# The memory's norm and transposes computed early, stored feature-major in DRAM and reloaded at the end of the mixers

## The chip, the cores and the metric

The kernel runs on one core of one Trainium2 chip. The metric is the device time of one execution in microseconds; each kernel is run three times and the median counts. A profile is one more execution, recorded by the chip's profiler.

## The reference

Two blocks run after each other on 512 tokens of width 1024, in fp32. The first block has two layers of four mixers (gated linear recurrences, a gated delta rule and a latent attention), an output projection and a gated feed-forward network (FFN). The second block has a layer A and a layer B, and each of them has, beside its own attention, a memory attention over 256 tokens `mem` that do not depend on anything the first block computes:

```python
def memory_attention(qm, mem, l, mem_norm, mem_w_kv, mem_q_norm, mem_k_norm):
    kvm = rms_norm_2(mem, mem_norm[l]) @ mem_w_kv[l]
    km, vm = jnp.split(kvm, 2, axis=-1)
    km = rms_norm_2(km.reshape(B, M, MEM_HEADS, MEM_HEAD_DIM), mem_k_norm[l])
    ...
```

Here M is 256, the width of `mem` is 1024, and `mem_w_kv[l]` is 1024 x 512. What the change touches is the first line: the norm of `mem`, and its transposition into the layout in which TensorE can multiply it with `mem_w_kv`.

## The kernel before

A product of fp32 matrices is made of three fp32r products: each operand is split into a high part `hi` (a ScalarE copy to fp32r) and the rest `lo` (a VectorE subtraction), and hi·hi, lo·hi and hi·lo are added in PSUM. Weights arrive by DMA into `wr` (512 KB each), ScalarE casts them to `wh`, VectorE subtracts to `wl`. Activations are split the same way after a transpose on TensorE (`tr`, into the PSUM pool `psS` or `psD`). All DMAs are issued by SyncE (SP), one after the other.

Every operation is first recorded, in program order, and then a planner sets a fixed order on each engine by list scheduling: among the operations that it takes to be ready it prefers the one that comes first in the program, and it gives each tile a slot of its pool (`p4w` has 16 slots of 4 KB a partition, `p4h` 8, `p4p` 8, `wr` 2, `wh` 4, `wl` 4, `psA` 3, `psS` 3, `psD` 2). The chip then runs each engine's list in that order. All recorded instructions carry the line of the helper that emits them, L328, so they are told apart by their tiles. SP's list is fixed in the same way, so a DMA that waits for its data holds up those behind it.

A first_block layer l (`layer1`) runs: `next_norm` with the first three weights of `w_in` (`fm_first`), then the mixers as a list of items in the order gdn, gate_d, hgrn, gla, mla, gate_a, gate_b, mem, then the output projection with `w_out`, then `next_norm` and `ffn`. The items `mem` come last. They prepare the memory of second-block layer l: `mem_h` loads the norm's gain row and the two 128-token tiles of `mem` (512 KB each), normalizes each (`norm_tok`: a ScalarE square with accumulation, four small POOL operations for the pair, a VectorE scale by row and gain), transposes it (8 TensorE transposes per tile into two `psS` tiles) and splits what comes out (a ScalarE copy and a VectorE subtraction of 512 columns per `psS` tile). Then `i_tm` multiplies with `mem_w_kv`: two token tiles of keys and two of values, each with 24 matmuls of 256 columns, 96 in all. `away` stores keys and values to DRAM (`md`), and layers A and B fetch them with `mem_back`.

Of the kernel before, what the change touches and what calls it, by code (L numbers as in the profile page):

```python
# [10 lines left out]
F32 = mybir.dt.float32  # L11
F32R = mybir.dt.float32r
U32 = mybir.dt.uint32
I32 = mybir.dt.int32
AF = mybir.ActivationFunctionType
# [132 lines left out]
def run(gen):  # L148
    for _ in gen:
        pass  # L150
# [463 lines left out]
class Net:  # L614
    def __init__(self, ctx, tc, I, out, dbg=None, upto=None):
# [20 lines left out]
        self.pps = {"A": pool("psA", 3, space=PSUM), "S": pool("psS", 3, space=PSUM), "D": pool("psD", 2, space=PSUM)}  # L636
        self.pdr = pool("pdr", 2, space=bass.MemoryType.DRAM)
        self.turn = 0
        self.ready_w, self.mem_kv = {}, {}
        self.ahead = lambda: None  # L640

    def nm(self, s):
# [1227 lines left out]
    def ffn(self, l, h, rest, then):  # L1870
# [13 lines left out]
            return self.fm(h, w)  # L1884

        for f in range(NF):
            psg, psu = proj(2 * f), proj(2 * f + 1)
            c = self.p2()
            self.act(c, psg, AF.Copy, scale=self.fcols[l](f, 2))
            for j in (1, 0):  # L1890
                s = 2 - j
                self.stt(c[:, s:], psg[:, :S - s], self.fcols[l](f, j), c[:, s:], ALU.mult, ALU.add)
            self.act(c, c, AF.Gelu_apprx_tanh)
            self.mul(c, psu, c)
            a = self.p4([128, 2, S], F32R, "w" if f < 16 else "p")
            self.split(a[:, 0, :], a[:, 1, :], c)
            acts.append(a)
# [6 lines left out]
    def layer1(self, l, steps):  # L1904
# [12 lines left out]
        gla, gate_b = self.gla_items(l, W, h, TB)  # L1917
        mla = self.mla_items(l, W, h, TC)
        mem = self.mem_items(l)
        self.merge(self.project(gdn + gate_d + hgrn + gla + mla + gate_a + gate_b + mem))  # L1920
        gb = self.bcast_row(I["post_mix_g"][l], D)
        mt = self.mixT
# [88 lines left out]
                self.mul(self.rot[:, i, t].rearrange("p w (b d) -> p w b d", b=2), g4,  # L2011
                         tab[:, t * 8:(t + 1) * 8].unsqueeze(1).unsqueeze(1).broadcast_to([128, 2, 2, 8]), self.G)

    def mem_h(self, l, h):

        I = self.I
        gb = self.bcast_row(I["mem_norm_2"][l], D)
        h.extend([self.p4([128, 4, 256], F32R) for _ in range(2)] for _ in range(2))
        for t in range(2):
            xn = self.p4()  # L2020
            raw = self.p4()
            self.SP.dma_start(out=raw, in_=I["mem_2"][0, t * 128:(t + 1) * 128, :])
            self.norm_tok(raw, gb, xn)
            yield self.when(xn)
            for g in range(2):
                ps = self.ps("S")
                for k in range(4):
                    self.tr(ps[:, k * 128:(k + 1) * 128], xn[:, (g * 4 + k) * 128:(g * 4 + k + 1) * 128])
                self.split(h[0][g][:, :, t * 128:(t + 1) * 128], h[1][g][:, :, t * 128:(t + 1) * 128],
                           ps.rearrange("p (k n) -> p k n", k=4))  # L2030

    def mem_items(self, l):

# [490 lines left out]
```

## Time and profile before

| what | us |
| --- | --- |
| three runs | 2032.98, 2035.56, 2035.82 (median 2035.56) |
| the profiled execution | 2033.99 |
| its span | 2032.2 |
| TensorE (PE) busy in it | 1954.1 (96%), mean granted clock 0.987 |
| VectorE (DVE) busy | 1250.3 (62%) |
| ScalarE (ACT) busy | 946.6 (47%) |
| GpSimd (POOL) busy | 265.7 (13%) |

The span is the part of the profiled execution in which instructions run; the other 1.8 us lie around it. Busy times of engines overlap. PEclk is the granted clock of TensorE as a share of its full 2.4 GHz; 0.50 is its lower level, 1.2 GHz. In a row of the timeline, the number in brackets is the time for which the engine stood idle before the instruction, and behind the arrow stands what released it. Consecutive matmuls of one kind share one row (x8), and their ends are modelled, so starts are the safer numbers.

### The profile page before, as it was taken

To read this page: it belongs to the slowest core of one execution; us is meant where nothing else is said; L and a number is where in the kernel's file an instruction comes from. 1 tells how busy PE (TensorE), PEld (TensorE's weight loads), DVE (VectorE), ACT (ScalarE), POOL (GpSimd) and SP (SyncE) were. 2 spreads that over 40 slices of the span, in tenths; PEclk is the share of its full clock that TensorE was granted. 3 is DMA by queue.
4 is the path that set the end of the run, shared out by engine and by line. 5 is a ranking of instruction groups with operands and counts; after the bars stand their busy time and mean duration, and the time that the engine had idled before them with its cause. 6 is when DMAs were issued, how large, how long until landed. Compare 5 with 4: busy or idle time off the path is not lost.

```text
span 2032.2 us, 33173 instructions
## 1 busy us (share of the span) xinstructions
PE 1954.1 (96%) x13254; PEld 1655.6 (81%) x13254; DVE 1250.3 (62%) x2319; ACT 946.6 (47%) x1715; POOL 265.7 (13%) x362
## 2 busy tenths in 40 slices
PE   7999989899999989998898999999999999999999
PEld 6888778788888878887787888888899988888787
DVE  7688873544442257878836444422548886558796
ACT  5744463433332236633634333322446774457782
POOL 3101111000000021011201000000223220005131
PEclk9999989999999999999999999999999999999999
DMA  5321224433332433302243333324331213421121
GB/s 166 97 63 36 83 81 138 125 94 94 98 99 94 155 90 96 92 24 68 82 152 112 100 94 94 99 97 167 121 89 43 84 63 114 135 84 55 60 74 62
DMA packets 231305, 191.62 MB, mean 94 GB/s; under 512 B 22352, under 2 KB 201200, under 8 KB 231152
## 3 DMA queue, kind: packets, MB, share of 16 engines
q1 hardware_dynamic: 231152, 189.51, 30.4%
q8 instruction: 104, 1.70, 0.3%
q14 instruction: 49, 0.40, 0.1%
HBM read 174.28 MB, written 15.20 MB: 93 GB/s over the span
## 4 chain that ended last, share of the span: by engine, by line
PE 84%; DVE 7%; ACT 3%; POOL 2%; issue 2%; DMA 1%; SPq 1%; DVEq 0%; ACTq 0%; POOLq 0%
PE psA L328 63%; PE psS L328 12%; PE psD L328 9%; DVE p4w L328 5%; POOL st L328 2%; ACT p4w L328 1%; DVE p4p L328 1%; DVE wl L328 1%; SPq L328 1%; DVE p L328 1%; ACT wh L328 0%; DMA wr<-in_w_in_dram 0%; ACT p4p L328 0%; ACT p L328 0%; DVE p4h L328 0%
## 5 line engine op out<-in xcount | busy, mean ns | idle before, releaser
L328 PE MATMUL psA<-p4h,wh 128*128 128x512 f32 (+1 forms) x2144 | 627.9, 377 | 14.3 <-DVE p4h L328 7.1
L328 DVE TENSOR_TENSOR wl<-wr,wh 128x1024 fp32r<-128x1024 f32 (+6 forms) x304 | 349.0, 1152 | 413.7 <-ACT wh L328 408.4
L328 ACT CAST wh<-wr 128x1024 fp32r<-128x1024 f32 (+6 forms) x304 | 298.5, 990 | 465.2 <-PE psA L328 279.8
L328 PEld LDWEIGHTS psA<-p4h,wh 128*128 128x128 f32 x2144 | 393.5, 191 | 89.9 <-DVE p4h L328 8.3
L328 PE MATMUL psA<-p4h,wl 128*128 128x512 f32 (+1 forms) x1072 | 400.6, 374 | 0.0
L328 PE MATMUL psA<-wh,p4h 128*128 128x256 f32 (+1 forms) x1792 | 353.8, 289 | 0.9 <-DVE p4h L328 0.7
L328 PEld LDWEIGHTS psA<-wh,p4h 128*128 128x128 f32 x1792 | 282.3, 188 | 6.6 <-issue 2.0
L328 PE MATMUL psA<-wl,p4h 128*128 128x256 f32 (+1 forms) x896 | 257.5, 288 | 0.4 <-DVE wl L328 0.4
L328 PEld LDWEIGHTS psA<-p4h,wl 128*128 128x128 f32 x1072 | 204.3, 191 | 37.0
L328 POOL TENSOR_SCALAR st<-st 128x1 f32<-128x1 f32 (+4 forms) x108 | 46.1, 427 | 1310.6 <-ACT p4w L328 908.5
L328 PEld LDWEIGHTS psA<-wl,p4h 128*128 128x128 f32 x896 | 168.8, 188 | 2.6 <-DVE wl L328 0.8
L328 PE MATMUL psA<-wh,p4w 128*128 128x512 f32 (+1 forms) x540 | 159.4, 368 | 0.0
L328 ACT ACTIVATE p<-p 128x512 f32<-128x512 f32 (+2 forms) x174 | 87.3, 526 | 100.2 <-DVE p L328 98.9
L328 POOL TENSOR_TENSOR st<-st,c 128x1 f32<-128x1 f32 (+4 forms) x106 | 115.4, 1090 | 8.0
L328 ACT ACTIVATE p4w<-psA 128x256 f32<-128x256 f32 (+5 forms) x138 | 61.6, 452 | 107.0 <-PE psA L328 105.9
L328 PEld LDWEIGHTS psA<-wh,p4w 128*128 128x128 f32 x540 | 96.6, 188 | 18.2 <-issue 0.5
L328 PE MATMUL psS<-consts,p4w 128*128 128x128 f32 (+1 forms) x448 | 70.5, 291 | 36.7 <-DVE p4w L328 28.9
L328 PE MATMUL psS<-p4w,p4w 128*64 128x64 f32 (+9 forms) x800 | 94.6, 271 | 5.3 <-DVE p4w L328 5.1
L328 PE MATMUL psA<-wl,p4w 128*128 128x512 f32 (+1 forms) x270 | 98.5, 365 | 0.0
L328 PE MATMUL psS<-wh,p4w 128*128 128x512 f32 x300 | 97.3, 395 | 0.0
L328 DVE TENSOR_TENSOR p<-psA,p 128x512 f32<-128x512 f32 x54 | 37.3, 691 | 95.8 <-PE psA L328 94.2
L328 PEld LDWEIGHTS psS<-consts,p4w 128*128 128x128 f32 x448 | 54.5, 153 | 47.7 <-issue 19.1
(227 smaller groups left out, 3105.0 us busy)
## 6 DMA issues: line engine op xcount, KB each, us to landing
wr<-in_w_in_dram SPq DMA_DIRECT2D x44, 512.0 KB, 3.8
wr<-in_ffn_w_gate_dram SPq DMA_DIRECT2D x44, 512.0 KB, 3.8
wr<-in_ffn_w_up_dram SPq DMA_DIRECT2D x44, 512.0 KB, 3.8
wr<-in_ffn_w_down_dram SPq DMA_DIRECT2D x44, 512.0 KB, 3.5
wr<-in_w_out_dram SPq DMA_DIRECT2D x16, 512.0 KB, 4.7
wr<-in_a_w_in_dram SPq DMA_DIRECT2D x16, 512.0 KB, 3.8
wr<-in_b_w_in_dram SPq DMA_DIRECT2D x16, 512.0 KB, 3.9
p4w<-xd SPq DMA_DIRECT2D x12, 512.0 KB, 4.4
```

The costliest lines, as they stand in the source:

```text
L328: op.fn(*op.args, **op.kw)
```

## The change

The norm and the transposes of the memory move out of `mem_h` into a new function `mem_prep(l)`. There ScalarE alone copies the transposed tiles out of PSUM, unsplit, into two fp32 tiles `hT` (128 x 4 x 256 each), and SP stores both to DRAM (`mh`, 512 KB each). `mem_prep(0)` is put into the list of items behind the first gdn item of layer 0, which the planner can start at the beginning of the program; `mem_prep(1)` runs in layer 0's FFN, at its third block of 128 hidden columns (f = 2). What is left in `mem_h` loads the two halves from `mh` and splits each (one ScalarE copy and one VectorE subtraction of 1024 columns).

```diff
@@ ffn
         for f in range(NF):
+            if l == 0 and f == 2:
+                run(self.mem_prep(1))
             psg, psu = proj(2 * f), proj(2 * f + 1)
@@ layer1
         mem = self.mem_items(l)
+        if l == 0:
+            gdn[1:1] = [self.i_do(lambda: self.mem_prep(0))]
         self.merge(self.project(gdn + gate_d + hgrn + gla + mla + gate_a + gate_b + mem))
@@
-    def mem_h(self, l, h):
+    def mem_prep(self, l):
 
         I = self.I
         gb = self.bcast_row(I["mem_norm_2"][l], D)
-        h.extend([self.p4([128, 4, 256], F32R) for _ in range(2)] for _ in range(2))
+        hT = [self.p4([128, 4, 256]) for _ in range(2)]
         for t in range(2):
...
                 for k in range(4):
                     self.tr(ps[:, k * 128:(k + 1) * 128], xn[:, (g * 4 + k) * 128:(g * 4 + k + 1) * 128])
-                self.split(h[0][g][:, :, t * 128:(t + 1) * 128], h[1][g][:, :, t * 128:(t + 1) * 128],
-                           ps.rearrange("p (k n) -> p k n", k=4))
+                self.act(hT[g][:, :, t * 128:(t + 1) * 128], ps.rearrange("p (k n) -> p k n", k=4), AF.Copy)
+        self.mem_hT[l] = []
+        for g in range(2):
+            d = self.pdr.tile([128, 4, 256], F32, tag=f"mh{l}{g}", name=self.nm("mh"))
+            self.SP.dma_start(out=d, in_=hT[g])
+            self.mem_hT[l].append(d)
+
+    def mem_h(self, l, h):
+
+        h.extend([self.p4([128, 4, 256], F32R) for _ in range(2)] for _ in range(2))
+        for g in range(2):
+            raw = self.p4([128, 4, 256])
+            self.SP.dma_start(out=raw, in_=self.mem_hT[l][g])
+            yield 0.0
+            self.split(h[0][g], h[1][g], raw)
```

Since the planner makes the order, the diff does not show where the operations land. The following rows do.

**The end of layer 0's mixers, TensorE.** In the list of before, `psS_624` and `psS_632` are attention scores, `psD_...<-consts,p` are transposes of softmax rows, `psS_663` and `psS_665` transpose the gla mixer's output, and `psS_656`, `psS_657` (and, further on, `667` and `668`) transpose the normalized memory `p4w_645`; the key products begin with `psA_675`, after all of them:

```order
L328 MATMUL psD_631<-consts_96,p_513_608 128x128
L328 MATMUL psD_637<-consts_96,p_520_615 128x128 x2
L328 MATMUL psS_632<-p4w_449,p4w_447 128x512
L328 MATMUL psS_632<-c_144,c_143 128x128
L328 MATMUL psS_663<-consts_96,p4w_495 128x128 x4
L328 MATMUL psS_656<-consts_96,p4w_645 128x128 x4
L328 MATMUL psS_657<-consts_96,p4w_645 128x128 x3
L328 MATMUL psD_652<-consts_96,p_532_627 128x128 x3
L328 MATMUL psD_653<-consts_96,p_540_635 128x128 x4
L328 MATMUL psS_657<-consts_96,p4w_645 128x128
L328 MATMUL psS_665<-consts_96,p4w_495 128x128 x3
```

In the list of after, `psA_673`, `psA_685` and `psA_689` are two key tiles and a value tile, of which two matmuls each stand ahead of the last score (`psS_651`); `p4w_659` is hi and `p4w_661` lo of the reloaded memory's first half, `p4w_660` and `p4w_662` hi and lo of its second half:

```order
L328 MATMUL psA_685<-wl_617,p4w_659 128x256
L328 MATMUL psA_689<-wh_668,p4w_659 128x256
L328 MATMUL psA_689<-wl_669,p4w_659 128x256
L328 MATMUL psS_651<-p4w_468,p4w_466 128x512
L328 MATMUL psS_651<-c_144,c_143 128x128
L328 MATMUL psA_673<-wh_616,p4w_661 128x256
L328 MATMUL psA_673<-wh_616,p4w_659 128x256
L328 MATMUL psA_673<-wl_617,p4w_659 128x256
L328 MATMUL psA_673<-wh_616,p4w_661 128x256
L328 MATMUL psA_673<-wh_616,p4w_659 128x256
L328 MATMUL psA_673<-wl_617,p4w_659 128x256
L328 MATMUL psA_673<-wh_616,p4w_661 128x256
```

The memory's 16 transposes are gone from here, and the rest of the first key tile (22 matmuls) now stands directly behind the last score, ahead of the transposes of gla and softmax. The other key and value matmuls come after those.

**The same place, VectorE.** Before, `p4w_495` is the gla output, multiplied by its gate and by its norm's factor; `p4w_645` and `p4w_658` are the two normalized memory tiles:

```order
L328 TENSOR_REDUCE st_633<-psS_632 128x1
L328 TENSOR_TENSOR p4w_495<-p4w_495,p4p_289 128x1024
L328 TENSOR_SCALAR st_634<-st_633 128x1
L328 TENSOR_TENSOR p4w_495<-p4w_495,st_651 128x1024
L328 SCALAR_TENSOR_TENSOR p4w_645<-p4w_646,st_649,p4w_640 128x1024
L328 SCALAR_TENSOR_TENSOR p4w_658<-p4w_659,st_662,p4w_640 128x1024
L328 RECIPROCAL st_628<-st_628 128x1
L328 RECIPROCAL st_636<-st_636 128x1
```

After, with `p4w_514` as the gla output, the two subtractions that make lo (`p4w_661`, `p4w_662`) stand around the product with the norm's factor:

```order
L328 TENSOR_REDUCE st_652<-psS_651 128x1
L328 TENSOR_TENSOR p4w_514<-p4w_514,p4p_308 128x1024
L328 TENSOR_SCALAR st_653<-st_652 128x1
L328 TENSOR_TENSOR p4w_661<-p4w_663,p4w_659 128x1024
L328 TENSOR_TENSOR p4w_514<-p4w_514,st_665 128x1024
L328 RECIPROCAL st_647<-st_647 128x1
L328 TENSOR_TENSOR p4w_662<-p4w_666,p4w_660 128x1024
```

The two scalings of the memory have left this place and two subtractions of 1024 columns have come, the first of them one place earlier in the list.

**The start of the program, SP and ScalarE.** `wsm` holds the narrow columns of `w_in` and is the third weight of `fm_first`. SP before:

```order
L328 DMA p_47_142<-in_neg_dram 128x384
L328 DMA p_914_1009<-in_plam_dram 128x256
L328 DMA st_1013<-in_positions_dram 128x4x1
L328 DMA wr_154<-in_wsm_dram 128x8x56
L328 DMA wr_168<-in_w_in_dram 128x8x128
L328 DMA wr_172<-in_w_in_dram 128x8x128
```

SP after:

```order
L328 DMA p_47_142<-in_neg_dram 128x384
L328 DMA p4w_172<-in_mem_norm_dram 128x1024
L328 DMA p4w_176<-in_mem_dram 128x1024
L328 DMA p4w_183<-in_mem_dram 128x1024
L328 DMA p_939_1034<-in_plam_dram 128x256
L328 DMA st_1038<-in_positions_dram 128x4x1
L328 DMA wr_154<-in_wsm_dram 128x8x56
L328 DMA wr_168<-in_w_in_dram 128x8x128
L328 DMA wr_191<-in_w_in_dram 128x8x128
```

Three loads of 512 KB now stand ahead of `wsm` and of the next `w_in` weights. ScalarE before, where `wh_155` is the cast of `wsm` in six pieces:

```order
L328 CAST c_144<-p_47_142 128x384
L328 CAST wh_155<-wr_154 128x8x56
L328 CAST wh_155<-wr_154 128x8x8
L328 CAST wh_155<-wr_154 128x8x32
L328 CAST wh_155<-wr_154 128x8x16 x2
L328 CAST wh_169<-wr_168 128x1024
```

ScalarE after:

```order
L328 CAST c_144<-p_47_142 128x384
L328 ACTIVATE st_1244<-bc_140 128x4
L328 ACTIVATE p4w_175,st_177<-p4w_176 128x1024
L328 ACTIVATE st_148<-st_148 128x4
L328 ACTIVATE p4w_182,st_184<-p4w_183 128x1024
L328 CAST wh_155<-wr_154 128x8x56
L328 CAST wh_155<-wr_154 128x8x8
L328 CAST wh_155<-wr_154 128x8x32
```

The two squares of the memory's norm (`p4w_175`, `p4w_182`) stand ahead of the casts of `wsm`. Of the 16 transposes of `mem_prep(0)`, 3 stand in the second half of `fm_first` on TensorE and 13 directly behind it; the two stores to `mh` stand on SP between the fifth and the sixth load of `w_in` weights. In layer 0's FFN, `mem_prep(1)` has its 16 transposes in the first blocks and its two stores between loads of FFN weights; its three loads stand on SP in layer 0's output projection, behind the third `w_out` weight.

## Rows read from the trace of the kernel before

**Rows 1.** The profile's page: TensorE's busy time, and the chain's shares by engine

```profile
PE 1954.1 (96%) x13254; PEld 1655.6 (81%) x13254; DVE 1250.3 (62%) x2319; ACT 946.6 (47%) x1715; POOL 265.7 (13%) x362
...
PE 84%; DVE 7%; ACT 3%; POOL 2%; issue 2%; DMA 1%; SPq 1%; DVEq 0%; ACTq 0%; POOLq 0%
```

**Rows 2.** Windows of 4 us, end of layer 0's mixers, with columns

```profile
core 0: us, PE busy (x) PEld busy (x) DVE busy (x) ACT busy (x) POOL busy (x), PEclk, DMA share, GB/s
280.00:284.00 4.00, 1.26 (x4) 0.49 (x3) 4.00 (x8) 3.97 (x6) 0.00 (x0) 1.00 0.75 246
284.00:288.00 4.00, 1.36 (x6) 1.02 (x7) 2.86 (x4) 3.97 (x10) 3.30 (x4) 0.63 0.05 18
288.00:292.00 4.00, 3.28 (x16) 2.88 (x15) 3.69 (x8) 1.53 (x5) 0.28 (x1) 0.50 0.01 4
292.00:296.00 4.00, 3.92 (x16) 1.58 (x16) 0.69 (x3) 0.84 (x2) 0.00 (x0) 0.59 0.00 0
```

**Rows 3.** TensorE's timeline there: start, us, what, [idle before, releaser]

```profile
285.72 1.09 PE L328 MATMUL psS<-consts,p4w 128*128 128x128 f32 x4 [3.31 <-DVE p4w L328]
...
297.29 0.37 PE L328 MATMUL psA<-wh,p4w 128*128 128x256 f32 x1
...
308.57 0.52 PE L328 MATMUL psA<-wh,p4w 128*128 128x256 f32 x2
```

**Rows 4.** Timeline, VectorE, same place

```profile
283.09 1.23 DVE L328 TENSOR_TENSOR p4w<-p4w,p4p 128x1024 f32<-128x1024 f32 x1
...
284.35 1.22 DVE L328 TENSOR_TENSOR p4w<-p4w,st 128x1024 f32<-128x1024 f32 x1
286.30 1.29 DVE L328 SCALAR_TENSOR_TENSOR p4w<-p4w,st,p4w 128x1024 f32<-128x1024 f32 x1 [0.73 <-POOL st L328]
```

**Rows 5.** TensorE's timeline in layer 0: eight transposes, a softmax-value product

```profile
266.69 1.73 PE L328 MATMUL psA<-p4w,p4w 128*64 128x512 f32 x8
268.24 0.82 PE L328 MATMUL psA<-p,p4w 128*64 128x256 f32 x8
...
278.00 1.04 PE L328 MATMUL psS<-consts,p4w 128*128 128x128 f32 x8
```

**Rows 6.** Timeline, VectorE and TensorE, the same in layer 1

```profile
1007.29 1.23 DVE L328 TENSOR_TENSOR p4w<-p4w,p4p 128x1024 f32<-128x1024 f32 x1
...
1009.92 1.08 PE L328 MATMUL psS<-consts,p4w 128*128 128x128 f32 x4 [3.31 <-DVE p4w L328]
...
1032.41 0.52 PE L328 MATMUL psA<-wh,p4w 128*128 128x256 f32 x2
```

**Rows 7.** Windows of 3 us at the start, columns as in rows 2

```profile
12.00:15.00 3.00, 1.12 (x4) 0.72 (x4) 2.40 (x3) 2.44 (x8) 1.55 (x2) 1.00 1.02 405
15.00:18.00 3.00, 1.54 (x8) 1.54 (x8) 2.86 (x8) 2.97 (x7) 1.70 (x3) 1.00 1.12 268
```

**Rows 8.** Timeline, ScalarE, VectorE and TensorE, third weight at the start

```profile
19.30 2.38 ACT L328 CAST wh<-wr 128x448 fp32r<-128x448 f32 x6
...
23.07 0.26 DVE L328 TENSOR_TENSOR wl<-wr,wh 128x128 fp32r<-128x128 f32 x1
...
25.48 0.40 PE L328 MATMUL psA<-p4h,wh 128*128 128x256 f32 x2
```

**Rows 9.** Windows: mixers' middle, FFN's start and FFN's inside, layer 0

```profile
160.00:200.00 40.00, 37.46 (x545) 33.20 (x546) 32.19 (x62) 16.72 (x39) 6.66 (x16) 1.00 0.16 44
364.00:368.00 4.00, 4.00 (x25) 4.00 (x24) 3.94 (x7) 1.39 (x3) 1.07 (x2) 0.63 0.76 255
400.00:440.00 40.00, 40.00 (x177) 32.81 (x176) 17.98 (x21) 14.46 (x19) 0.00 (x0) 1.00 0.33 96
```

**Rows 10.** Timeline, VectorE and TensorE, layer 0's output projection

```profile
310.93 2.54 DVE L328 TENSOR_TENSOR wl<-wr,wh 128x1024 fp32r<-128x1024 f32 x2 [3.21 <-ACT wh L328]
...
319.89 0.39 PE L328 MATMUL psA<-wh,p4w 128*128 128x512 f32 x1
```

**Rows 11.** Part 6 of the page, DMA issues: count, KB each, us to landing

```profile
wr<-in_w_in_dram SPq DMA_DIRECT2D x44, 512.0 KB, 3.8
```

More of the change, by code (lines that the diff above doesn't have):

```diff
@@ L638, in __init__ @@
         self.turn = 0
-        self.ready_w, self.mem_kv = {}, {}
+        self.ready_w, self.mem_kv, self.mem_hT = {}, {}, {}
         self.ahead = lambda: None
```

## The prediction

> **What bounds the kernel now.** The profile's page comes first: TensorE is busy for 96% of the span, and 84% of the chain that ended last runs on it [rows 1]. So only what adds work to TensorE, or opens or closes one of its gaps, can move the time; work on other engines counts where TensorE waits for it. Next I looked for the gaps in the windows. One lies where the change removes work, at the end of layer 0's mixers: from 280 to 288 us TensorE does 1.26 and 1.36 us of work in 4 us each while VectorE and ScalarE are nearly full, and the granted clock falls to 0.63, then 0.50, then 0.59, and TensorE works at the lower level of 1.2 GHz [rows 2]. TensorE's timeline names the wait: 3.31 us before 285.72, released by VectorE [rows 3]. VectorE's timeline shows what it had to do by then: two products of 1024 columns on the gla output and then the memory's two scalings, each held up for a further 0.73 us by POOL, with the second like the first shown [rows 4]. The 96 key and value matmuls of the memory start only at 297.29 and end at 308.57, so each takes 11.28/96 = 0.1175 us at full clock [rows 3]. Layer 1 has the same gap of 3.31 us, and its key and value matmuls end at 1032.41 [rows 6]. These matmuls are long, need nothing of the gla output, and wait only because the memory's norm and transposes stand last. That is the room the change can use.
>
> **The change, part by part.** *End of layer 0's mixers.* Here 16 transposes, two scalings, two squares and eight splits of 512 columns go; two casts and two subtractions of 1024 columns come. On VectorE the gla gate product still ends at 283.09 + 1.23 = 284.32 [rows 4]. Behind it stands the first lo subtraction, which I price like the neighbouring product of the same shape at 1.22 us [rows 4]: with 0.1 us for a small operation between them it ends at 285.6, and the first key tile can go on at about 285.7. Its first ten matmuls use the first half of the memory; the eleventh or so needs the second lo, which comes 1.22 + 0.1 + 1.22 us after the first, at 288.2. Ten matmuls take 1.2 us at full clock and about twice that at half, so TensorE waits again until 288.2 either way. From there 80 of the 96 matmuls remain (six are done in the gap, ten before 288.2): 80 x 0.1175 = 9.4 us. Seven transposes of softmax rows and eight of the gla output remain too, at 1.04/8 = 0.13 us [rows 5]: 2.0 us. The softmax-value product takes 1.73 + 0.82, less the overlap of their starts, about 2.3 us [rows 5]. With no half clock after 288.2 the stage ends at 288.2 + 13.7 = 301.9 instead of 308.57: 6.7 us gained. How long will the clock stay low? At the FFN's start, where TensorE comes out of a gap into dense matmuls, the window reads 0.63, which is 0.37/0.5 = 74% of 4 us, or 3.0 us, at half [rows 9]; from 285.7 that reaches to 288.7, and costs 0.3 us behind 288.2. In before's own restart the three windows give 3.0 + 4.0 + 3.3 = 10.2 us at half [rows 2]; from 285.7 that reaches to 295.9 and costs half of 7.7 us, 3.9 us. The new restart is dense but for one short wait, so I take the first: 6.4 us gained, with 2.8 and 6.7 as bounds.
>
> What the Trainium skill says of this stands apart: "TensorE: Matmul & The Clock Gate", section "HAM oscillation — how this bites in real kernels", describes kernels whose waits for data repeatedly put TensorE's clock to half, so that a gap costs more than its own length. The trace agrees, 0.50 behind the gap [rows 2]; by that rule the clock falls here also after the change, for the gap before 285.7 stays, and the bound of 6.7 us would not be reached.
>
> *Layer 1* has the same lists. Its gate product ends at 1007.29 + 1.23 = 1008.52 [rows 6], so the second lo is there at 1012.4, and the stage ends at 1012.4 + 13.7 + 0.3 = 1026.4 instead of 1032.41: 6.0 us gained, with 2.4 and 6.3 as bounds by the same reasoning.
>
> *FFN of layer 0.* The second 16 transposes come to a TensorE that has no idle time, 40.00 of 40 us [rows 9]: 16 x 0.13 = 2.1, less where they overlap their neighbours, so +1.9 us (1.4 to 2.5). ScalarE's squares and four copies and VectorE's scalings are hidden: these engines work 14.46 and 17.98 of 40 us there [rows 9]. If that cover were gone, an FFN weight would be late by as much, some 4 us.
>
> *Start.* The 16 transposes cost +2.1 us here also, and 1.57 MB now stand ahead of the third weight. In the rows the queue moved 405 and 268 GB/s [rows 7], which makes 3.9 to 5.9 us. Before, the third weight's casts run from 19.30 to 21.68, VectorE ends its low parts at 23.3, and TensorE uses them at 25.48 [rows 8]. Pushed back, the casts end at 25.6 to 27.6 and the low parts at 27.2 to 29.2: TensorE waits some 1 to 3.5 us, as the squares (which stand ahead of these casts) are done while the weight is still landing. Part of it can be taken up later, where TensorE waits for other engines that meanwhile went on: in the mixers' middle it is idle for 2.54 of 40 us [rows 9]. I take +2.0 us in all, with 0 and +5.3 as bounds.
>
> *Middle of both layers' mixers.* New tiles in `p4w` shift slots and order there. I count 0, bounded by its idle time on either side: 2.5 us per layer [rows 9].
>
> *Output projection of layer 0.* The loads of layer 1's memory come behind the third `w_out` weight. That weight's and the fourth's low parts are ready at 313.47, and the third is first used at 319.89 [rows 10]; the fourth is needed later still, so more than 6.4 us of slack stand against at most 5.9 us of transfer: 0.
>
> The sum on the profiled execution of 2033.99 us: -6.4 - 6.0 + 1.9 + 2.0 = -8.5, so 2025.5. That execution lies 1.6 us below the median of the three runs, and inside their spread; I say 2025 us. A difference under 0.2%, some 4.1 us, can hardly be told from none here.
>
> **The rivals.** *Better:* the clock does not drop behind the gap (6.7 + 6.3), the start is wholly absorbed (0), the FFN costs 1.4 and the middles tighten by 2.5 each: -16.6, or 2017 us. For it speaks that TensorE's gap becomes shorter; against it the clock rule above and that a new order has no reason to be better twice.
>
> *The wait only changes its owner:* the keys wait for VectorE's subtractions where the transposes waited for its scalings, and TensorE works at half clock as long as now. Then the layers give 2.8 + 2.4, and -5.2 + 1.9 + 2.0 = -1.3 makes 2032.7. For it speaks that the first wait stays as long as it was, to within 0.1 us; against it that behind it stand 22 matmuls of one kind and not groups of four and seven.
>
> *The first half pays it back:* the start costs its far end, 5.3, and the tighter slots add 2.5 us of idle time in each layer's middle: -8.5 + 3.3 + 5.0 = -0.2, 2033.8. For it speaks that every `p4w` slot has users already; against it that the weights' casts have slack of 3.8 us at the start [rows 8].
>
> *Slower:* SP's queue is held up. The stores to `mh` stand between weight loads and can only go when the last of the 16 transposes has been copied out; until then SP issues none of the weights behind them. If a weight is late by its whole way, its transfer of 3.8 us [rows 11] and a cast and a subtraction of 1024 columns, at 1.2 us each like the product in [rows 4], TensorE stands for 6 us and starts again at half clock, 1.5 us more. In the first mixer and in the FFN that is 15 us: -8.5 + 15 = +6.5, 2040.5. The change breaks even where these holds come to 8.5 us together. Against it speaks that TensorE in the FFN finds its weights without a wait over 40 us while the transfers take a third of the time [rows 9].
>
> **How the numbers follow.** The forecast gets 0.62, better 0.12, the changed owner 0.10, the payback 0.08 and the slower case 0.08. The forecast's own bounds reach from 2020 to 2030. Faster by over 0.2% are the forecast and the better case, 0.74; within 0.2% the changed owner and the payback, 0.18; slower 0.08. The range from 2017 to 2033 takes in the better case and most of the changed owner, and leaves out under 2 in 10. The single value is that of the forecast.
>
> **What would show it.** In the changed profile the key matmuls should start at once behind the last score, with a wait for VectorE of some 3 us, and then a second one of up to 1.3 us; the output projection should begin 6 us earlier after the start of its stage in both layers; the granted clock should be back at 1.00 about 4 us after the restart and not 12. The third weight at the start should land 4 to 6 us later, and TensorE show a wait of 1 to 3.5 us before it; the FFN should be longer by 1.9 us with no new gap. The prediction is wrong if the key matmuls wait at half clock for longer, if ScalarE's cast of the reloaded memory comes late, if TensorE waits for `w_in` or FFN weights behind a store to `mh`, or if the mixers' middles, which I took as unchanged, move by more than 2.5 us each.

## The result, and the profile after

The changed kernel runs in 2025.03 us (median of four runs, 2024.29 to 2025.99), against 2035.69 us for the kernel before in runs beside it. The ratio is 0.9948 with a 95% interval from 0.9932 to 0.9963, which is 10.6 us (7.5 to 13.8). The forecast was 2025 us and a range from 2017 to 2033. The profiled execution took 2024.52 us with a span of 2021.6 us, 10.6 us less than the span of before.

The page first: TensorE's busy time fell by 2.9 us only (before in [rows 1]), so 7.7 of the 10.6 us that went are time in which it was idle.

```profile
span 2021.6 us, 33187 instructions
...
PE 1951.2 (97%) x13254; PEld 1658.7 (82%) x13254; DVE 1249.8 (62%) x2315; ACT 948.3 (47%) x1718; POOL 262.3 (13%) x362
```

The windows at the end of layer 0's mixers, after the change, answer to [rows 2]; the columns are the same.

```profile
278.00:282.00 4.00, 2.47 (x14) 1.55 (x12) 4.00 (x8) 3.97 (x7) 0.00 (x0) 1.00 0.69 206
282.00:286.00 4.00, 1.95 (x9) 1.95 (x10) 4.00 (x6) 3.39 (x6) 0.00 (x0) 0.50 0.15 58
286.00:290.00 4.00, 4.00 (x26) 4.00 (x26) 1.64 (x5) 0.82 (x2) 0.00 (x0) 0.65 0.00 0
290.00:294.00 4.00, 4.00 (x34) 3.30 (x34) 3.70 (x10) 2.33 (x5) 1.21 (x2) 1.00 0.09 13
```

The gap is still there, and the clock still falls to 0.50, the level of 1.2 GHz. But from 286 us on TensorE is full, and by 290 us the clock is back. TensorE's timeline of the same place answers to [rows 3]:

```profile
279.71 1.12 PE L328 MATMUL psS<-p4w,p4w 96*128 96x512 f32 x2 [0.43 <-DVE p4w L328]
...
284.05 0.80 PE L328 MATMUL psA<-wh,p4w 128*128 128x256 f32 x2 [3.16 <-DVE p4w L328]
...
288.70 0.34 PE L328 MATMUL psA<-wh,p4w 128*128 128x256 f32 x1
288.88 1.04 PE L328 MATMUL psS<-consts,p4w 128*128 128x128 f32 x8
```

Behind the last score TensorE waits 3.16 us, where it had waited 3.31 us; now it is the first key tile that waits. That tile runs without a break to 288.88, 22 matmuls in 4.8 us, 0.22 us each, nearly twice the 0.1175 us of the full clock. VectorE's timeline, as in [rows 4], shows what it waits for:

```profile
281.58 1.23 DVE L328 TENSOR_TENSOR p4w<-p4w,p4p 128x1024 f32<-128x1024 f32 x1
...
282.79 1.21 DVE L328 TENSOR_TENSOR p4w<-p4w,p4w 128x1024 fp32r<-128x1024 f32 x1
283.92 1.22 DVE L328 TENSOR_TENSOR p4w<-p4w,st 128x1024 f32<-128x1024 f32 x1
...
285.13 1.21 DVE L328 TENSOR_TENSOR p4w<-p4w,p4w 128x1024 fp32r<-128x1024 f32 x1
```

The gla gate product ends, the first lo is made in 1.21 us, and TensorE starts at its end, 284.0. The second lo is there at 286.34, and TensorE, at half clock, gets to it at about that time.

Where the 10.6 us went is shown best by the stages. Each length below is the difference between the starts of two TensorE instructions that stand in both kernels: the first 512-column matmul behind `fm_first`, the last score of 384 columns in the mixers, the first matmul of the output projection, the first 512-column matmul in the FFN behind its `fm_first`, the first of the FFN's down projection, and the same in layer 1. For both kernels there are two profiled executions, the second from the experiments below. The stages at the start and at the FFN's start end ahead of some of the added transposes: of the first 16, 12 lie in the start's stage and 4 in the next; of the second 16, 3 lie in the stage ahead of the FFN's and 13 in the FFN's.

| stage, us | before | before, again | after | after, again | mean change | forecast |
| --- | --- | --- | --- | --- | --- | --- |
| start to `fm_first`'s end | 39.72 | 39.41 | 40.84 | 40.64 | +1.2 | +2.0 |
| layer 0 mixers to the last score | 239.48 | 241.48 | 236.85 | 237.15 | -3.5 | 0 |
| from there to the output projection | 29.49 | 29.55 | 23.26 | 23.39 | -6.2 | -6.4 |
| output projection, FFN's start | 75.38 | 75.43 | 76.13 | 76.17 | +0.7 | 0 |
| layer 0 FFN | 286.83 | 286.84 | 288.28 | 288.28 | +1.4 | +1.9 |
| down projection, layer 1's start | 92.88 | 92.90 | 93.70 | 93.74 | +0.8 | 0 |
| layer 1 mixers to the last score | 239.62 | 238.25 | 237.94 | 238.21 | -0.9 | 0 |
| from there to the output projection | 29.12 | 29.80 | 23.71 | 23.48 | -5.9 | -6.0 |
| output projection, FFN's start | 75.26 | 75.56 | 76.16 | 76.16 | +0.7 | 0 |
| layer 1 FFN | 286.84 | 286.84 | 286.83 | 286.84 | 0.0 | 0 |
| the rest (layers A and B) | 637.59 | 638.12 | 637.93 | 639.02 | +0.6 | 0 |

### The profile page after: what moved, and what is told of

It reads as the page before. It is cut to its first block, busy times and chain, and to the rows that moved or that the text cites. A ratio compares the mean times of both kernels' runs of the same rounds, so it can differ in the third digit from the quotient of the medians.

```text
span 2021.6 us, 33187 instructions
## 1 busy us (share of the span) xinstructions
PE 1951.2 (97%) x13254; PEld 1658.7 (82%) x13254; DVE 1249.8 (62%) x2315; ACT 948.3 (47%) x1718; POOL 262.3 (13%) x362
## 5 line engine op out<-in xcount | busy, mean ns | idle before, releaser
L328 POOL TENSOR_SCALAR st<-st 128x1 f32<-128x1 f32 (+4 forms) x108 | 41.7, 386 | 1290.9 <-ACT p4w L328 880.2
L328 PE MATMUL psA<-wh,p4w 128*128 128x512 f32 (+1 forms) x540 | 164.4, 376 | 6.3 <-DVE p4w L328 6.3
```

Source lines behind the costliest of these rows:

```text
L328: op.fn(*op.args, **op.kw)
```

## The experiments

The theory was the forecast's: each mixers' end gains for itself, about 6 us, since the long key matmuls need nothing of the gla output and only stood behind the memory's own preparation; the early work costs little at the start and in the FFN. The main rivals were that the gain comes from wherever the clock's half stretches happen to fall, that the wait only changes its owner, and, new at this point, that the early computation is not needed at all, as the order alone was at fault. The kernel before ran beside each group; its medians there were 2035.3 to 2035.9 us.

| kernel | median, us | ratio to before (95%) | us by the ratio |
| --- | --- | --- | --- |
| the change, again | 2024.23 | 0.9947 (0.9933 to 0.9961) | -10.8 |
| the kernel before, again | 2035.56 | 0.9999 (0.9991 to 1.0008) | -0.2 |
| only the first memory early | 2025.62 | 0.9961 (0.9947 to 0.9975) | -7.9 |
| only the second memory early | 2032.42 | 0.9989 (0.9980 to 0.9999) | -2.2 |
| only the norm early | 2032.33 | 0.9978 (0.9967 to 0.9988) | -4.5 |
| first memory behind the gdn items | 2028.57 | 0.9967 (0.9956 to 0.9979) | -6.7 |
| first memory behind gdn and its gate | 2035.28 | 0.9996 (0.9988 to 1.0005) | -0.8 |
| first memory behind the gla items | 2018.31 | 0.9913 (0.9900 to 0.9926) | -17.7 |
| lo on POOL | 2024.59 | 0.9945 (0.9933 to 0.9958) | -11.2 |
| before, memory item one place earlier | 2020.04 | 0.9920 (0.9904 to 0.9937) | -16.3 |
| change, reload and split one place earlier | 2016.32 | 0.9909 (0.9890 to 0.9927) | -18.5 |
| the same, with only the second memory early | 2014.89 | 0.9899 (0.9886 to 0.9912) | -20.6 |

Single runs of one kernel lie up to some 9 us apart (the kernel before 2031.5 to 2040.8), more than for the changed one (2023.1 to 2026.0); differences under 2 us between these rows say little. A profile is one such execution, and five of them lie far from their kernel's median: only the first memory early 6.7 us above it (2032.34) and only the second 3.8 above (2036.18); first memory behind the gla items 3.6 below (2014.74), lo on POOL 3.4 below (2021.14) and the kernel before with the item one place earlier 3.8 below (2016.29). Stage lengths of these carry that much chance.

**Both kernels once more, for a second profile.**

> The kernel before, once more, for a second profile. Theory: the order is fixed, so the stretches of half clock lie where they lay, at the same lengths: one in the middle of layer 0's mixers, two in layer 1's, 10.2 us at both mixers' ends, 6.8 us at the FFNs' starts. Rival: the short ones in the middles come and go from one execution to the next, then the 2.5 and 1.7 us by which the middles were shorter after the change are not the change's.

> The changed kernel, once more, for a second profile. Theory: the stretches of half clock lie where they lay: none in the middle of layer 0's mixers, 6.8 us at both mixers' ends, 10.2 us at both FFNs' starts. Rival: the 10.2 us at the FFNs' starts (6.8 before) come and go between executions, and then the 0.8 us that each FFN start cost are not the change's.

The ends repeat: half clock at the same places, the stage lengths within 0.7 us (table above). The middle of layer 0's mixers does not. In the first profile of before the clock fell near 224 us:

```profile
220.00:224.00 4.00, 2.73 (x37) 1.98 (x36) 3.90 (x7) 2.41 (x4) 2.67 (x4) 0.95 0.02 6
224.00:228.00 4.00, 4.00 (x28) 2.38 (x28) 3.85 (x8) 1.57 (x3) 0.00 (x0) 0.63 0.00 0
```

In the second it fell at another place, near 236 us, and for longer, and the stage took 2.0 us more:

```profile
236.00:240.00 4.00, 4.00 (x30) 3.54 (x30) 0.78 (x4) 0.92 (x4) 0.00 (x0) 0.50 0.14 49
240.00:244.00 4.00, 4.00 (x57) 3.71 (x56) 0.69 (x1) 0.00 (x0) 0.00 (x0) 0.69 0.42 131
```

After the change, in both profiles, the clock stays at 1.00 there, though the gap is no smaller (2.36 us busy in 4):

```profile
220.00:224.00 4.00, 2.36 (x23) 1.75 (x23) 3.87 (x7) 1.30 (x3) 1.21 (x2) 1.00 0.00 0
224.00:228.00 4.00, 4.00 (x42) 3.00 (x41) 3.88 (x8) 3.35 (x7) 0.00 (x0) 1.00 0.05 7
```

So the rival is half right. These short falls come and go between executions of one program, and the 0.9 us in layer 1 are within that; that layer 0 lost them in both profiles is in favour of the change, but two of two is not much, and in the profile of the next kernel, with the same work in layer 0, the clock fell near 224 us (0.83 and 0.74 in these two windows), and the stage took 238.8 us. A longer half clock where TensorE starts again behind the projections is in both profiles of the change and in neither of before.

**One memory at a time.** The first kernel leaves the call for layer 1 out of the FFN and prepares that memory as before; the second leaves out the item in layer 0.

```diff
-            if l == 0 and f == 2:
+            if l == 0 and f == -1:
                 run(self.mem_prep(1))
```

```diff
-            gdn[1:1] = [self.i_do(lambda: self.mem_prep(0))]
+            pass
```

> Only the first memory's norm and transposes are made early; the second memory is prepared at the end of layer 1's mixers as before. Theory (each mixers' end gains for itself): the end of layer 0 gives 6.2 us, its start costs 1.1, the FFN costs nothing, layer 1's end is as before; the middle of layer 0's mixers keeps its 2.5 us if the earlier norm causes it. 2028 to 2030.5 us against 2035.7 before. Rival (the gains come from where the clock's half stretches happen to fall in a new order): the middle of layer 0 does not show 2.5 us, and the total may lie anywhere from 2026 to 2034.

> Only the second memory's norm and transposes are made early, in layer 0's FFN; the first is prepared at the end of layer 0's mixers as before, and nothing is added at the start. Theory: the end of layer 1's mixers gives 5.4 us, the FFN costs 1.5, layer 1's middle keeps its 1.7 us if the change causes it: 2030 to 2032 us against 2035.7. The gains of this kernel and of the one with the first memory alone add up to that of the change, within 2 us. Rival (chance of the clock's stretches): they don't add up, by more than 2 us.

Both medians missed their expected ranges: 2025.62 is below 2028 to 2030.5, and 2032.42 just above 2030 to 2032. By the ratios the two add up: -7.9 and -2.2 make -10.1, against -10.6 for the change. This is a loose test, as the intervals are 5.1 to 10.8 and 0.2 to 4.1 us, and by the medians it would be some -13.7: the first kernel's seven runs lie at 2025.1 to 2025.6 and at 2030.4 to 2032.3, with nothing between. The ends are the better evidence. Layer 0's end took 23.47 us with the first memory alone, as after the change, and 29.41 with the second alone, as before; layer 1's end took 27.33 and 22.92. So each end gains for itself, though layer 1's end was 1.8 to 2.5 us shorter than before with the first memory alone too, where nothing was changed in it. With the second memory alone the gain of 6.5 us at layer 1's end is mostly given back ahead of it, in the execution profiled: that stage took 243.07 us, 3.5 to 4.8 more than before, for the clock fell twice and for longer there:

```profile
928.00:932.00 4.00, 4.00 (x21) 3.78 (x18) 3.87 (x9) 0.69 (x1) 0.00 (x0) 0.50 0.66 228
...
952.00:956.00 4.00, 4.00 (x22) 2.56 (x23) 3.83 (x8) 0.45 (x1) 0.00 (x1) 0.58 0.02 4
```

**The norm early, the transposes where they were.** `mem_prep` stores the normalized rows; `mem_h` reloads them, transposes and splits as before.

```diff
             yield self.when(xn)
+            d = self.pdr.tile([128, 1024], F32, tag=f"mh{l}{t}", name=self.nm("mh"))
+            self.SP.dma_start(out=d, in_=xn)
...
```

> The norm alone is made early and stored token-major; the 16 transposes and the 512-column splits of each layer stay at the mixers' end. Theory (what holds TensorE up is VectorE with the memory's scalings, and its transposes in small groups behind them): half of the gain goes, the transposes find the normalized rows early but the splits still take ScalarE and VectorE in the gap; 2028 to 2031 us. Rival (only the norm's chain over ScalarE, POOL and VectorE was late; the transposes fill a gap that TensorE has anyway): as good as the change or better, as no transposes are added to the FFN and the start, 2021 to 2025 us.

The theory is borne out, though with less than its range: 4.5 us, and 26.98 and 25.90 us at the ends, against 29.1 to 29.8 before and 23.3 to 23.7 after. Eight transposes now fill part of the gap, but then their splits stand in it:

```profile
281.93 1.31 PE L328 MATMUL psS<-consts,p4w 128*128 128x128 f32 x8 [1.15 <-DVE p4w L328]
284.57 0.39 PE L328 MATMUL psA<-wh,p4w 128*128 128x256 f32 x1 [1.33 <-ACT p4w L328]
287.05 2.08 PE L328 MATMUL psS<-p4w,p4w 96*128 96x512 f32 x2 [1.73 <-ACT p L328]
```

**The memory's item one place earlier.** In both kernels only the place in the program changes: the item that fetches the memory and makes hi and lo stands ahead of the gla gate's projection (the tiles for keys and values are still taken where they were). The first starts from the change, the second from the kernel before, which then stores and reloads nothing.

```diff
-... gla + mla + gate_a + gate_b + mem))
+... gla + mla + gate_a + mem[:1] + gate_b + mem[1:]))
```

> The change, with the reload and the split of the memory put one item earlier in the program, ahead of the gla gate's projection, so that the planner puts them ahead of the gla output's gate product on ScalarE and VectorE. Theory (what is left of the gap is TensorE's wait of 3.16 us for VectorE's first lo, and the half clock behind it): both layers lose the wait and about 2.4 us of half clock, 5.5 us each, 2014 us. Rival (the wait only changes its owner: the gla transposes or the softmax stand last, and the key matmuls run out before): within 2 us of the change, 2023 to 2027.

> The kernel before, with nothing of the change; only the item that loads, normalizes, transposes and splits the memory stands one place earlier in the program, ahead of the gla gate's projection. No early computation and no way through DRAM. Theory of the change (the norm and the transposes must leave the mixers' end): the memory's operations still sit among the softmax and gla operations on ScalarE and VectorE and delay them, 2025 to 2032 us. Rival (only the order was bad: they stood behind the gla output on VectorE although their data were there): as good as the change or better, 2014 to 2025 us, since the transposes then fall where TensorE had idled and nothing is stored.

The first gained most of what its theory has, 2016.32 us against 2014: the two ends are 4.3 and 3.5 us shorter than after the change, where 5.5 each were expected. The second went to its rival's side: 16.3 us are gained with the order alone, without any early work, against 18.5 with both, and these two differ by less than their intervals. In either, TensorE is full at the end of layer 0's mixers, and the clock stays at 1.00. First the change with the reload earlier, then the kernel before with the item earlier:

```profile
277.00:281.00 4.00, 4.00 (x28) 3.25 (x27) 3.33 (x11) 2.29 (x8) 0.00 (x0) 1.00 0.17 39
281.00:285.00 4.00, 4.00 (x38) 4.00 (x37) 3.79 (x7) 3.98 (x7) 0.00 (x0) 1.00 0.71 229
285.00:289.00 4.00, 4.00 (x31) 2.62 (x30) 3.19 (x5) 2.48 (x5) 0.96 (x1) 1.00 0.85 260
```

```profile
278.00:282.00 4.00, 4.00 (x38) 4.00 (x37) 3.95 (x14) 3.96 (x12) 0.00 (x0) 1.00 0.01 4
282.00:286.00 4.00, 4.00 (x33) 2.70 (x31) 3.70 (x5) 3.77 (x6) 0.00 (x0) 1.00 0.11 10
```

What the change left at the ends was thus the wait of 3.16 us and the half clock behind it, and both are gone once lo is made before the gla output's product instead of behind it. The last kernel of this kind keeps the early order for both memories, and the way through DRAM for the second alone:

> The item that prepares the memory stands ahead of the gla gate's projection in both layers; only the second memory's norm and transposes are made early, in the FFN, and nothing is added at the start. Theory (terms add): layer 0 as in the kernel with the order alone, layer 1 as in the kernel with the reload and the early order; the start's 1.1 us come back: 2014 to 2018 us. Rival (the early norm of the first memory is needed to keep layer 0's mixers dense): 2018 to 2021 us.

Its 2014.89 us are the lowest of all and in the theory's range; from the kernel with both memories early and the item earlier (2016.32) the intervals don't tell it apart.

**Lo on POOL.** The two subtractions leave VectorE's list; TensorE's list at layer 0's end stays the same.

```diff
-            self.split(h[0][g], h[1][g], raw)
+            self.split(h[0][g], h[1][g], raw, eng=self.G)
```

> The change, with the memory's two lo subtractions per layer on POOL instead of VectorE; TensorE's list at the mixers' end stays as it is. Theory (the 3.16 us wait is for the place of the first lo behind the gla gate product in VectorE's list, and the half clock follows from the wait): POOL, which is idle there, has the lo before TensorE asks for it or 1 to 2 us after, the wait shrinks to 0 to 1.5 us, the clock stays up or falls for less; 3 to 5 us gained per layer, 2015 to 2019 us. Rival (the clock falls for the sparse work ahead of the wait, or the keys then wait for something else): under 1.5 us per layer, 2022 to 2025.

The total is the rival's, by a way that neither had. In layer 0 POOL makes the first lo well before it is asked for, from 277.06 on, and the wait of 3.16 us is gone. But while POOL works, VectorE's operations of two tiles in SBUF take nearly three times as long:

```profile
277.06 2.36 POOL L328 TENSOR_TENSOR p4w<-p4w,p4w 128x1024 fp32r<-128x1024 f32 x1 [10.55 <-DVE wl L328]
283.52 2.99 POOL L328 TENSOR_TENSOR p4w<-p4w,p4w 128x1024 fp32r<-128x1024 f32 x1 [4.10 <-ACT p4w L328]
```

```profile
277.17 3.34 DVE L328 TENSOR_TENSOR wl<-wr,wh 128x1024 fp32r<-128x1024 f32 x1 [0.19 <-ACT wh L328]
...
284.31 3.28 DVE L328 TENSOR_TENSOR p4w<-p4w,st 128x1024 f32<-128x1024 f32 x1
```

The weights' subtraction (1.23 us in the change) takes 3.34, the gla product (1.22) 3.28, and TensorE waits behind these instead:

```profile
281.22 1.13 PE L328 MATMUL psS<-p4w,p4w 96*128 96x512 f32 x2 [2.54 <-DVE p4w L328]
...
287.74 0.95 PE L328 MATMUL psS<-consts,p4w 128*128 128x128 f32 x7 [1.51 <-DVE st L328]
```

In layer 1 the theory's gain does show. There POOL makes the first lo already at 969.21, TensorE's one wait at the end is 1.18 us, the clock stays at 1.00, and the end takes 19.36 us, 4.2 less than after the change. The middle ahead of it, where the clock fell twice, took 241.06 us, 3 more than after the change; whether that belongs to the kernel or to this execution is not shown. So the total, equal to that of the change, hides that the theory holds in one of the two layers.

**The first memory at three other places.** The item `mem_prep(0)` moves from the program's start to behind the first mixer's items (gdn), behind these and their gate, or behind the gla items. The edit of the last is shown.

```diff
-            gdn[1:1] = [self.i_do(lambda: self.mem_prep(0))]
+        P = [self.i_do(lambda: self.mem_prep(0))] if l == 0 else []
-        self.merge(self.project(gdn + gate_d + hgrn + gla + mla ...
+        self.merge(self.project(gdn + gate_d + hgrn + gla + P + mla ...
```

> The change, with the first memory's norm and transposes placed behind the first mixer's items instead of at the program's start. Theory (the start pays for 1.57 MB ahead of the third weight and for 16 transposes): the start's 1.1 us come back, the transposes cost up to 1.9 us in the mixers unless they fall into gaps; 2023.5 to 2026 us. Rival (the start costs nothing for itself and the middle of the mixers is full): slower by 1 to 3 us, 2026 to 2028.

> The change, with the first memory's norm and transposes placed at the end of the first mixer's items, one step earlier than in the kernel that lost the whole gain. Theory A (work placed inside the mixers always costs): 2030 to 2036 us. Theory B (that loss was of one place): 2022 to 2026 us.

> The change, with the first memory's norm and transposes placed behind the gla items, two mixers later than in the kernel that lost the whole gain. Theory A (work placed inside the mixers always costs, as VectorE and ScalarE wait there in fixed order and each gap lets the clock fall): 2030 to 2036 us. Theory B (that loss was of one place, where the planner's new order fell badly; elsewhere the transposes cost 1 to 2 us and the start's 1.1 come back): 2022 to 2026.

The start's cost came back, at the second place only in part: `fm_first` ends at 38.29, 40.00 and 39.44 us, in this order, against 40.84 and 40.64. What the rest does was missed by both sides, for the places differ by 17 us. Behind gdn and its gate the whole gain is lost: layer 0's mixers from `fm_first` to the output projection take 267.3 us, nearly as long as before (269.0 and 271.0; the change 260.1 and 260.5), and the output projection's stage (79.3) and layer 1's mixers (241.4) take 3 us more each than after the change. Behind gdn alone they take 266.4. In both the gap at layer 0's end is closed, with 0.2 us of idle time or less behind the last score of 384 columns; the loss lies in the middle. TensorE is idle there for 14.8 us, and 11.1 behind gdn alone, against 8.2 after the change, in waits for small products of the recurrences, and the clock falls. These rows are of the place behind the gate, where the clock of the change stays at 1.00 in both windows:

```profile
206.97 0.89 PE L328 MATMUL psD<-p4w,p4w 64*64 64x64 f32 x8 [1.45 <-DVE p4w L328]
...
211.85 0.45 PE L328 MATMUL psD<-p4w,p4w 64*64 64x64 f32 x2 [1.60 <-DVE p4w L328]
```

```profile
200.00:210.00 10.00, 6.92 (x63) 5.53 (x61) 8.38 (x29) 1.01 (x2) 0.00 (x0) 0.86 0.35 107
210.00:220.00 10.00, 8.31 (x74) 6.38 (x72) 6.84 (x12) 1.96 (x3) 0.00 (x0) 0.63 0.16 53
```

Behind the gla items the same stretch takes 254.1 us, 6 less than after the change, and 2018.31 us in all. There TensorE waits nowhere for more than 0.4 us between 270 us and the output projection: the gap at the end is gone, with the memory's items still last in the program. In the planner's new order lo is made long before the gla gate product, the last of these rows, as in the kernels with the item one place earlier:

```profile
238.92 1.23 DVE L328 TENSOR_TENSOR p4w<-p4w,p4w 128x1024 fp32r<-128x1024 f32 x1
...
240.72 1.22 DVE L328 TENSOR_TENSOR p4w<-p4w,p4w 128x1024 fp32r<-128x1024 f32 x1
...
278.98 1.23 DVE L328 TENSOR_TENSOR p4w<-p4w,p4p 128x1024 f32<-128x1024 f32 x1
```

So this place refutes theory A, that work inside the mixers always costs. Theory B has it right that the loss depends on the place, but its range, 2022 to 2026, was missed at both places that tested it (2028.57 and 2018.31): the place decides more than the work that is moved. Why the planner's order falls badly at two of the three places was not tried.

## Why the prediction was right, step by step

*The ends* carry the gain, and they were sized within 0.2 us: -6.2 and -5.9 against -6.4 and -6.0. The order of events was as told: the gate product, lo 1.2 us behind it, keys at once. One step in it failed without showing in the sum. I had TensorE wait a second time, to 288.2, for the second lo, and at half clock for 3.0 us in all. In the trace there is no second wait. The half clock outlasts it: the first key tile runs at half from 284.05 to 288.7, 4.7 us, and takes the time in which the wait would have been. Behind the second lo, at 286.34, this costs 1.2 us, half of 2.4, where the sum had 0.3; on the other side the second lo came 0.3 us sooner behind the gate product than the sum had it. That the terms agree to 0.2 us is thus in part luck. (The eight splits that the forecast counts are four casts and four subtractions; nothing in its sum hangs on this.) The bound of before's own restart (10.2 us at half) was too high here; that restart is sparse [rows 2] and this one is not, and no run separates this from other differences.

By the Trainium skill, "TensorE: Matmul & The Clock Gate", section "HAM oscillation — how this bites in real kernels", a gap that drops the clock makes the matmuls behind it slow as well. The runs agree: behind the gap a key matmul took 0.22 us instead of 0.1175, and in the three kernels with the item one place earlier the gap of 3 us closed, the clock stayed at 1.00 at both ends, and they gain 16.3 to 20.6 us where the change gains 10.6.

*The FFN* came out at +1.4 (forecast +1.9), since 13 of the 16 transposes stand in its stage, at 0.11 us each; the other three stand just ahead of it. With the second memory alone, and in the kernel with the earlier reload, it grew by 0.6 us (287.4 against 286.8), as only five of the transposes stand in it there. The other eleven fall into the stage ahead of it, which was no longer than before with the second memory alone and 0.5 us longer in the other (75.2 and 75.9 us against 75.4). So a transpose costs 0.11 us where TensorE is full, and little in that stage, where TensorE was idle for 7 us.

*The start* was sized at +2.0 and measured +1.2. The step that failed is the wait for the third weight, 1 to 3.5 us by the sum (its own figures give 1.7 to 3.7). The weight did come as late as forecast: before, its load was issued at 14.23 us and took 4.3 to land, after the change it was issued at 16.94 and took 6.0, so it landed 4.4 us later in the first profiles. This ScalarE row is of the change, and answers to the first of [rows 8]:

```profile
22.96 1.42 ACT L328 CAST wh<-wr 128x448 fp32r<-128x448 f32 x5 [0.30 <-DMA wr<-in_wsm_dram]
```

The casts begin 3.7 us later. The row of before has six casts, and I took all six as this weight's; the ScalarE list of before, ahead of the prediction, shows five, and the sixth, of 1024 columns, is of the next weight. So the casts did not run to 21.68 but ended about 1 us sooner. The low parts came only 2.2 us later, and that is what the sum had wrong. Before, VectorE made them from 21.14 to 23.33 with other small operations between; after the change, when these were done, it made all five in one go, to 25.53. The first row is of before, the second of the change:

```profile
21.14 0.61 DVE L328 TENSOR_TENSOR wl<-wr,wh 128x448 fp32r<-128x448 f32 x1
```

```profile
24.04 1.49 DVE L328 TENSOR_TENSOR wl<-wr,wh 128x448 fp32r<-128x448 f32 x5
```

That is just when TensorE asks for them. In the first profile it did not wait at all; in the second it came to them sooner and waited 0.96 us:

```profile
25.61 0.38 PE L328 MATMUL psA<-p4h,wl 128*128 128x256 f32 x1 [0.96 <-DVE wl L328]
```

So the +1.2 us are those 12 of the 16 transposes that stand in this stage; nine of them take 0.9 us, from 39.94 to 40.84.

*The middles* were taken as unchanged, within 2.5 us. They gave 3.5 and 0.9. For layer 0 that is one of the forecast's own signs of being wrong. The bound was the idle time [rows 9], and that was the wrong price: the idle time ahead of TensorE's instructions in that stage adds up to 8.5 us before, in both profiles, and to 8.2 and 8.4 after. What differs is whether a gap drops the clock: before was at half for about 3.4 us in the first profile and 6.5 or more in the second, by the windows above, which costs 1.7 and at least 3.2 of the 2.6 and 4.3 us. That a new place could also cost 7 us, as in the kernels with the first memory behind gdn, my bound of 2.5 us did not allow for; the change happened to fall well.

*The stretches behind the projections* were not in the sum at all. They cost 0.7, 0.8 and 0.7 us, 2.3 in all. The clock is low there for longer than before, where it stood at 0.63 in the window that holds the restart [rows 9]. These are windows of the change at the start of layer 0's FFN:

```profile
352.00:356.00 4.00, 1.09 (x5) 0.72 (x5) 3.55 (x7) 1.89 (x4) 0.96 (x1) 0.50 0.67 191
356.00:360.00 4.00, 4.00 (x18) 4.00 (x19) 3.94 (x8) 1.79 (x3) 1.07 (x2) 0.50 0.64 222
360.00:364.00 4.00, 4.00 (x33) 4.00 (x33) 3.60 (x4) 0.00 (x0) 0.00 (x0) 0.94 0.50 142
```

The kernel with the first memory alone has the same longer fall at the FFN's start, without any memory work in that FFN, and so has the kernel before with the item one place earlier, without any early work at all. So it does not need the work that was put there; why the longer fall goes with some programs and not with others stays open.

*In sum* the time came out within 0.1 us of the forecast, and that is luck. The gain was forecast at 8.5 us and measured at 10.6. The forecast started from the profiled execution of before, 2033.99 us, which lies 1.7 below the median of 2035.69, and was rounded down by 0.5; together these cover the 2.1 us that the gain was short. The terms outside the two ends missed in both directions: the middles gave 4.4 us that were not counted, the stretches behind the projections took 2.3, the start and the FFN took 1.3 less than counted, and layers A and B, which are unchanged, took 0.6 more.

*The rivals.* The wait did change its owner, but only its first 3 us, not the sparse restart behind it. The queue held up by stores did not happen: layer 0's FFN is longer by its transposes and no more. The rival that I did not name is the one that counts: that the work need not move at all. The profile had it. This row of SP's timeline of before has the two loads of the memory's rows:

```profile
239.02 9.64 SPq L328 DMA_DIRECT2D p4w<-in_mem_dram  x2
```

They were issued by 249 us and took at most 3.7 us to land. The scalings, which stood behind the gla products in VectorE's list, ran from 286.30 on [rows 4], and on ScalarE too the squares that they need stood behind the gla gate:

```profile
282.00 1.06 ACT L328 ACTIVATE p4p<-p4p 128x1024 f32<-128x1024 f32 x1
...
283.22 1.05 ACT L328 ACTIVATE p4w<-p4w 128x1024 f32<-128x1024 f32 x1
```

Asking why they came so late, and not only how to be rid of them, leads to the 16 us of one moved item.

## What to carry to other kernels

When an engine's work stands last, look first at when its inputs were there. If they were there long before, move the work in the list, ahead of the operations that hold it up, before it is computed elsewhere and carried through memory. Price a gap by its own length and by the half clock behind it, and look at what follows the gap: here a gap of 3.3 us in front of sparse work meant 10.2 us at half clock, and one of 3.2 us in front of a dense key tile 6.8 (by the windows, the gap's own half clock included). Where a planner makes the order, the place of a new item can be worth more than the item, here 17 us between three places, so try several.

## What the hardware showed beyond that

VectorE and POOL hold each other up on operations that read two tiles in SBUF: VectorE's 1024 columns took 3.28 and 3.34 us instead of 1.22 and 1.23 while POOL's took 2.36 to 2.99 us beside them, about 2.1 us for each such overlap. The Trainium skill names this: "GPSIMD Engine Reference", section "1. Specifications", has the two engines share their SBUF interfaces, with contention for VectorE instructions that have two SBUF inputs. The traces agree. They show more than a slowdown: the operation that begins second ends as late as if it had waited for the whole of the first. These rows are of layer 1 with lo on POOL:

```profile
1003.64 3.45 POOL L328 TENSOR_TENSOR p4w<-p4w,p4w 128x1024 fp32r<-128x1024 f32 x1 [13.95 <-ACT p4w L328]
```

```profile
1003.63 1.23 DVE L328 TENSOR_TENSOR p4w<-p4w,st 128x1024 f32<-128x1024 f32 x1
1004.78 3.38 DVE L328 TENSOR_TENSOR wl<-wr,wh 128x1024 fp32r<-128x1024 f32 x1
```

VectorE's product, which began first, took its usual 1.23 us, and POOL's subtraction took 3.45 instead of 2.36. VectorE's next one ends at 1008.16, 1.07 us behind POOL's end at 1007.09; in layer 0 the two ends lie 1.08 and 1.09 us apart.

The same gap does not always drop the clock. One program, in two executions, fell near 224 us in the one and near 236 us in the other, for 2.0 us of difference in the stage; the changed kernel, with a gap as long near 222 us, did not fall there at all.
